# Layer 0's expert products in whole turns, and a staggered S5 loop, in a two-layer hybrid diffusion backbone

## The chip, the cores and the metric

The kernel runs on one core of one Trainium2 chip. The metric is the device time of one launch in microseconds, the median of three runs. TensorE multiplies, VectorE and ScalarE do most of the element-wise work, GpSimd does the rest of it and the indirect transfers, and SyncE issues nearly all loads. Each engine works through its own instructions strictly in the order in which they stand in the program; they wait for each other at semaphores.

## The reference

Two layers (DEPTH = 2), each a mixer followed by a mixture of experts, over 512 latent tokens and 256 context tokens of 1024 channels, all in float32. Layer 0 updates latents and context, layer 1 only the latents.

The mixer has four branches (attention, Mamba-2 SSD, S5, a gated short convolution) that are merged by sigmoid gates. The S5 branch has 24 groups of 16 inputs and 64 complex states, runs over the tokens in both directions, and is what the change touches:

```
ab_re, ab_im, bb_re, bb_im = s5_discretise(lam_re[d], lam_im[d], log_step[d], b_re, b_im)
h = complex_linear_scan(ab, s5_drive(u, bb))        # h[t] = ab*h[t-1] + bb@u[t], d = 1 on flipped tokens
y = Re(c @ (h_fwd + h_bwd)) + d_skip*u ;  y = gelu(y) ; y = y * sigmoid(y @ w_glu + b_glu)
```

The mixture is expert choice: each of 16 experts takes its best tokens, 64 of the latents and, in layer 0, 32 of the context.

```
aff = softmax(h @ w_router); gval, idx = top_k(aff.T, cap); xg = h[idx]
hid = silu(xg @ w_gate[e]) * (xg @ w_up[e]) ;  ye = (hid @ w_down[e]) * gval ;  out[idx] += ye
```

Each of the three weight matrices of an expert is 1024 x 1024, so 12 MiB are loaded for each expert and layer.

## The kernel before

**Experts.** `wtile()` loads half a matrix per tile `we`. There are two streams ("jobs"): latents (64 tokens, the 1024 output columns in 2 parts of 512) and, in layer 0, context (32 tokens, 4 parts of 256). The two tilings are "64-column" (2 parts at once beside each other in the array) and "32-column" (4 parts). `up()` (products on L1346) multiplies a stream by gate or up weights, 8 chunks of the inner dimension, k = 0 to 7. `hidden()` makes silu(g)*u on ScalarE and VectorE (L1357 to L1359), transposes it on TensorE (L1362) and copies it out of PSUM on ScalarE (hidT, L1364). `down()` multiplies by the down weights (L1376). Between them stand the gathers of the next tokens: `pick` (L1301) and the transposes of the gathered rows (L1332). In the code an expert (after expert 0) has gate for both streams, up for both streams, the hidden layers, then down for both.

PSUM has 8 banks, dealt among three groups by a triple: 'a', 'b', 'mm' (shown as psa, psb, psmm). `MIX = ((2, 3, 3), (3, 3, 2))` is that of the mixer of layers 0 and 1, `MOE` has the same numbers. In layer 0 an expert takes from group 'a' a bank for the latents' gate, one for both of the context's products, one for the latents' up, and one for the latents' down. `self.va(n, tag)` takes the next bank of a group, in turn; without a tag it is 'b' in S5.

**S5.** The loop `for g0 in range(0, 24, 4)` runs six times over four groups. In an iteration: the products Bx = B*powers (six GpSimd instructions, the helper's L995 to L1000) and Cx = C*powers (six on VectorE, the same lines; ScalarE negates one part, L1129); transposes of Bx (TensorE L1134, copied to Bt by ScalarE L1135); the short kernel matrix KK (TensorE L1143, sums L1147 to L1149 on ScalarE and VectorE), spread to T0 by DMA; the transposed inputs U (TensorE L1157, ScalarE L1158) and their copy in reversed order Ur (VectorE L1159, L1160); the driven inputs pv (TensorE L1165, L1166); the phase tables T (GpSimd, six instructions); H = T*pv (VectorE L1177 to L1182), the scan (VectorE L1185), S = the states turned back (VectorE L1192 to L1196); the readout y = T0*U + Cx*S (TensorE L1201, L1203), and its sum into u_tok (VectorE L1207). Every tile of the loop has one buffer, so the next iteration's T can be written only after the last L1193.

While S5 runs, TensorE also gets products of the input projections (L98 to L100, three for each product, in a split float32 form; fwL, L114 on VectorE, makes the low part of a weight) and of the modulation (L193 to L214). They fill TensorE between S5's own products.

**What sets the order.** The program is laid out when it is built. A scheduler goes through the instructions with a cost model of its own and appends to each engine's program the one that it holds ready first; the order in the code breaks ties. So the two streams of an expert, and the filling products of S5, stand in the order which that model finds, not in that of the code, unless a dependency is given by hand.

Of the kernel before, what the change touches and what calls it, by code (L numbers as in the profile page):

```python
# [9 lines left out]
F32 = mybir.dt.float32  # L10
# [45 lines left out]
MOE = ((2, 3, 3), (3, 3, 2))  # L56


class Kern:
# [942 lines left out]
    def s5(self):  # L1002
        nc, wp, par = self.nc, self.wp, self.par
# [113 lines left out]
        with self.pool("s5b") as bp:  # L1117
            W = lambda nm, *s: bp.tile([128, *s], F32, name=nm)
            for g0 in range(0, 24, 4):
                gg = slice(g0, g0 + 4)  # L1120

                Bx = [W(f"Bx{i}", 4, 8, 16) for i in range(2)]
                Cx = [W(f"Cx{i}", 4, 10, 16) for i in range(2)]
                z1, e1 = W("z1", 4, 10, 16), W("e1", 4, 8, 16)
                ap = lambda P, n, i: P[:, i, :, gg].rearrange("p s g -> p g s")[:, :, :, None].to_broadcast([128, 4, n, 16])
                av = lambda v, n: v[:, gg][:, :, None, :].to_broadcast([128, 4, n, 16])
                self.cmul(nc.gpsimd, Bx[0], Bx[1], ap(PB, 8, 0), ap(PB, 8, 1), av(bb[0], 8), av(bb[1], 8), e1)
                self.cmul(V, Cx[0], Cx[1], ap(PC, 10, 0), ap(PC, 10, 1), av(cc[:, 0], 10), av(cc[:, 1], 10), z1)
                nc.scalar.mul(Cx[1], Cx[1], -1.0)  # L1129
                Bt = [W(f"Bt{i}", 4, 128) for i in range(2)]  # L1130
                for i in range(2):
                    ps = self.va(512)
                    for q in range(4):
                        nc.tensor.transpose(ps[:, q * 128:(q + 1) * 128], Bx[i][:, q].rearrange("p s i -> p (s i)"), self.ident)  # L1134
                    nc.scalar.copy(Bt[i].rearrange("p a b -> p (a b)"), ps)  # L1135

                KK = bp.tile([16, 4, 15, 16], F32, name="KK")
                kf = [self.va(128).rearrange("p (d j) -> p d j", d=8) for _ in range(2)]
# [15 lines left out]
                U, Ur = W("U", 4, 96), W("Ur", 4, 96)  # L1154
                ps = self.va(384).rearrange("p (g b) -> p g b", g=4)
                for q in range(4):
                    nc.tensor.transpose(ps[:, q], u_tok[:, g0 + q].rearrange("p s i -> p (s i)"), self.ident[:96, :96])  # L1157
                nc.scalar.copy(U, ps)  # L1158
                V.tensor_copy(Ur[:, :, 0:32], U[:, :, 31::-1])  # L1159
                V.tensor_copy(Ur[:, :, 32:96], U[:, :, 95:31:-1])  # L1160
                pv = []
                for i in range(2):
                    p = self.va(384).rearrange("p (g b) -> p g b", g=4)
                    for q in range(4):
                        nc.tensor.matmul(p[0:64, q], Bt[i][:, q, 0:64], U[:, q], start=True, stop=True, skip_group_check=True)  # L1165
                        nc.tensor.matmul(p[64:128, q], Bt[i][:, q, 64:128], Ur[:, q], start=True, stop=True, skip_group_check=True)  # L1166
                    pv.append(p)

                T = [W(f"Tr{i}", 4, 6, 16) for i in range(2)]
                h4 = lambda i: hi[:, i, :, gg].rearrange("p a g -> p g a")[:, :, :, None].to_broadcast([128, 4, 6, 16])  # L1170
                l4 = lambda i: lo[:, i, 1:17, gg].rearrange("p a g -> p g a")[:, :, None, :].to_broadcast([128, 4, 6, 16])
                self.cmul(nc.gpsimd, T[0], T[1], h4(0), h4(1), l4(0), l4(1), e1[:, :, :6])
                T = [x.rearrange("p g a b -> p g (a b)") for x in T]

# [7 lines left out]
                V.tensor_sub(H[1], H[1], g2)  # L1182
# [468 lines left out]
```

## Time and profile before

| what | value |
|---|---|
| median of 3 runs | 3123.74 us (3120.9 to 3125.51) |
| profiled execution | 3125.83 us, of which the span of the trace 3124.1 us |
| TensorE (PE), VectorE (DVE), ScalarE, GpSimd busy | 2846.2, 1559.2, 783.8, 619.7 us (91, 50, 25, 20%) |
| granted TensorE clock, mean | 0.966 of full speed |
| bytes moved by DMA, mean rate | 659.79 MB, 211 GB/s |
| S5 loop of layer 0 and of layer 1 | 385 to 564.4 us, 2055 to 2241.8 us |
| experts of layer 0; experts 1 to 5; 6 to 15 | 1131.7 to 1733.4; 1172.3 to 1346.9; to 1733.4 us |
| experts of layer 1 | from about 2650 us to the end |

The stages follow each other in time: the projections, SSD and S5 of layer 0, attention, merge, experts, then the same for layer 1. The busy shares are averages over stages of different kinds. A row of windows has the stretch, its length, busy time and count of PE, PEld (weight loads, beside PE), DVE, ACT and POOL, the granted clock, the DMA share and GB/s. In a timeline the count of TensorE's float32 products is twice that of the program's instructions, as the trace has two records for each. What stands in brackets is the idle time ahead of an instruction and what ended it.

### The profile page before, as it was taken

The numbers are of one execution on the slowest core, as the hardware profiler recorded it, in microseconds if no ns is written. First come the engines' busy times: TensorE is split into PE (matmuls) and PEld (weight loads), VectorE is DVE, ScalarE is ACT, GpSimd is POOL, SyncE is SP. The second block draws the span as 40 slices with busy tenths as digits, with TensorE's granted clock in tenths as the row PEclk, the third lists the DMA queues.
The fourth block names the chain that finished last, engine by engine and source line by source line (L and its number), as shares of the span: only waits on it lengthen the run. The fifth ranks groups of instructions, "written<-read, shape, count | busy, mean of one in ns | idle before, by whom it ended". The sixth has DMA issues, their size and how long they took to land. (4 is left out here: it accounts for less than half of the span.)

```text
span 3124.1 us, 47057 instructions
## 1 busy us (share of the span) xinstructions
PE 2846.2 (91%) x18626; PEld 1826.3 (58%) x18626; DVE 1559.2 (50%) x3507; ACT 783.8 (25%) x1725; POOL 619.7 (20%) x765
## 2 busy tenths in 40 slices
PE   7999878999999979999999799977999896998887
PEld 4866756788888943433333376756687684332223
DVE  5477688555436552212111546798856565232223
ACT  4253222426522200000000332322436421000001
POOL 1022165120004121111110104065220031010001
PEclk9999999999999989999999899988999997999999
DMA  7324424311256479999996531432320486999998
GB/s 234 116 69 132 139 89 124 120 48 53 79 199 200 155 278 396 402 383 351 339 363 254 183 110 54 153 105 75 98 76 25 162 283 254 409 408 409 409 409 305
DMA packets 323039, 659.79 MB, mean 211 GB/s; under 512 B 22017, under 2 KB 191233, under 8 KB 322818
## 3 DMA queue, kind: packets, MB, share of 16 engines
q1 hardware_dynamic: 300688, 601.66, 53.6%
q10 hardware_dynamic: 15186, 32.93, 2.8%
q0 software_dynamic: 6944, 22.19, 2.3%
q8 instruction: 147, 2.41, 0.3%
q14 instruction: 74, 0.61, 0.1%
HBM read 602.85 MB, written 50.71 MB: 209 GB/s over the span
## 5 line engine op out<-in xcount | busy, mean ns | idle before, releaser
L1346 PE MATMUL psa<-we,X 128*64 128x512 f32 (+1 forms) x4096 | 605.1, 494 | 31.2 <-DMA we<-in_w_exp_gate_dram 15.8
L1346 PEld LDWEIGHTS psa<-we,X 128*64 128x64 f32 (+1 forms) x4096 | 193.7, 123 | 422.9 <-issue 318.7
L98 PE MATMUL psmm<-hH,fwH 128*128 128x512 f32 x984 | 374.1, 380 | 7.8 <-DVE xpad L636 3.6
L100 PE MATMUL psmm<-hH,fwL 128*128 128x512 f32 x984 | 368.3, 374 | 0.0
L99 PE MATMUL psmm<-hL,fwH 128*128 128x512 f32 x984 | 368.2, 374 | 0.0
L1376 PE MATMUL psa<-we,hidT 128*64 128x512 f32 x992 | 248.7, 609 | 21.3 <-ACT hidT L1364 14.9
L98 PEld LDWEIGHTS psmm<-hH,fwH 128*128 128x128 f32 x984 | 190.8, 194 | 51.4 <-issue 14.6
L1357 ACT ACTIVATE hid<-psa 128x512 f32<-128x512 f32 (+1 forms) x48 | 25.3, 526 | 779.1 <-PE psa L1346 739.3
L100 PEld LDWEIGHTS psmm<-hH,fwL 128*128 128x128 f32 x984 | 190.6, 194 | 30.7 <-issue 5.9
L99 PEld LDWEIGHTS psmm<-hL,fwH 128*128 128x128 f32 x984 | 191.1, 194 | 29.2 <-issue 6.1
L1381 DVE SCALAR_TENSOR_TENSOR y<-psa,ag,m 64x512 f32<-64x512 f32 x62 | 46.5, 750 | 274.0 <-PE psa L1376 273.4
L1376 PEld LDWEIGHTS psa<-we,hidT 128*64 128x64 f32 x992 | 67.8, 138 | 156.9 <-issue 112.5
L1359 DVE TENSOR_TENSOR hid<-hid,psa 128x512 f32<-128x512 f32 (+1 forms) x48 | 28.7, 597 | 252.1 <-PE psa L1346 251.8
L114 DVE TENSOR_TENSOR fwL<-fr,fwH 128x1024 fp32r<-128x1024 f32 (+1 forms) x100 | 117.1, 1172 | 73.4 <-ACT fwH L113 64.6
L471 POOL TENSOR_TENSOR merged<-merged,tgm 128x512 f32<-128x512 f32 (+1 forms) x48 | 62.8, 1326 | 424.0 <-DVE tgm L469 423.7
L1337 POOL TENSOR_TENSOR X<-X,modT 128x512 f32<-128x512 f32 x40 | 42.4, 1073 | 491.3 <-DVE X L1336 474.9
L1358 DVE SCALAR_TENSOR_TENSOR hid<-hid,psa 128x512 f32<-128x512 f32 (+1 forms) x48 | 28.7, 598 | 221.8 <-ACT hid L1357 221.8
L98 PE MATMUL psa<-cwH,hH 128*128 128x256 f32 (+1 forms) x432 | 122.1, 283 | 0.1
L113 ACT CAST fwH<-fr 128x1024 fp32r<-128x1024 f32 (+1 forms) x100 | 89.6, 897 | 128.2 <-DMA fr<-in_w_in_dram 62.1
L100 PE MATMUL psa<-cwH,hL 128*128 128x256 f32 (+1 forms) x432 | 121.6, 282 | 0.0
L99 PE MATMUL psa<-cwL,hH 128*128 128x256 f32 (+1 forms) x432 | 121.3, 281 | 0.0
L416 ACT ACTIVATE tg<-psmm 128x512 f32<-128x512 f32 x96 | 51.2, 533 | 160.4 <-PE psmm L100 152.8
(528 smaller groups left out, 5879.1 us busy)
## 6 DMA issues: line engine op xcount, KB each, us to landing
we<-in_w_exp_gate_dram SPq DMA_DIRECT2D x128, 1024.0 KB
we<-in_w_exp_up_dram SPq DMA_DIRECT2D x128, 1024.0 KB
we<-in_w_exp_down_dram SPq DMA_DIRECT2D x128, 1024.0 KB
fr<-in_w_mod_dram SPq DMA_DIRECT2D x96, 512.0 KB
fr<-in_w_in_dram SPq DMA_DIRECT2D x64, 512.0 KB
raw<-in_w_in_dram SPq DMA_DIRECT2D x36, 512.0 KB
gs<-tg ACTq DMA_DIRECT2D x32, 384.0 KB
tgm<-gs SPq DMA_DIRECT2D x32, 384.0 KB
```

The lines of the kernel that those rows point to most:

```text
L98: self.nc.tensor.matmul(ps, ah, bh, start=start and i == 0, stop=False)
L99: self.nc.tensor.matmul(ps, ah, bl, start=False, stop=False)
L100: self.nc.tensor.matmul(ps, al, bh, start=False, stop=stop and i == n - 1)
L113: self.nc.scalar.copy(h, x)
L114: self.nc.vector.tensor_sub(l, x, h.bitcast(F32))
L416: nc.scalar.activation(tg[:, o:o + n], self.cm(w, m, o, n), AF.Tanh, scale=0.5)
L471: (V if i == 3 else nc.gpsimd).tensor_add(dst, dst, t)
L1337: nc.gpsimd.tensor_add(X[:, hk], X[:, hk], Bm[:, 24 + h * 4:28 + h * 4, s:s + 1].to_broadcast([128, 4, 128]))
L1346: self.lastup = nc.tensor.matmul(ps[s][j * c:(j + 1) * c], X[s][:, k, r:r + c], w(k)[:, j * n:(j + 1) * n], start=k == 0, stop=k == 7, ski ...
L1358: V.scalar_tensor_tensor(hid, hid, 1.0, g, op0=OP.add, op1=OP.mult)
L1376: nc.tensor.matmul(ps[j * c:(j + 1) * c], lh, w(k)[:, j * n:(j + 1) * n], start=k == 0, stop=k == 7, skip_group_check=True)
L1381: V.scalar_tensor_tensor(Y[s][r, nn], ps[j * c:(j + 1) * c], got[s][1][r, e:e + 1], m5[s][r, nn], op0=OP.mult, op1=OP.mult)
```

## The change

Two parts, which share no instruction.

**Experts of layer 0.** `MOE[0]` becomes (4, 2, 2): four banks in group 'a', two in each of the others. Up now runs with the context ahead of the latents (`jobs[::-1]`), so that the 32-column products of gate and up follow each other. `behind()` adds a dependency that costs no semaphore (both instructions are TensorE's) and ties the first product of a turn behind the last product of the turn before, in gate, up and down.

**S5.** The iteration is split into `drive(g0)` (Bx, Bt, U, Ur, pv) and `matrices(g0)` (T, Cx, KK, T0). The drive of the next four groups is written right after H, ahead of the scan, and the next matrices right after the readout. U has two buffers. Ur is made by two ScalarE copies straight from PSUM, in reversed order, in place of VectorE's copies of U. The transposes of U and Bx, the products of KK and the readout take their banks from group 'a' (2 banks in layer 0, 3 in layer 1); pv stays in 'b'.

```diff
-MOE = ((2, 3, 3), (3, 3, 2))
+MOE = ((4, 2, 2), (3, 3, 2))
...
+            def drive(g0):
...
+                self.cmul(nc.gpsimd, Bx[0], Bx[1], ap(PB, 8, 0, gg), ap(PB, 8, 1, gg), av(bb[0], 8, gg), av(bb[1], 8, gg), e1)
+                U, Ur = bp.tile([128, 4, 96], F32, name="U", bufs=2), W("Ur", 4, 96)
+                ps = self.va(384, "a").rearrange("p (g b) -> p g b", g=4)
+                for q in range(4):
+                    nc.tensor.transpose(ps[:, q], u_tok[:, g0 + q].rearrange("p s i -> p (s i)"), self.ident[:96, :96])
+                nc.scalar.copy(U, ps)
+                nc.scalar.copy(Ur[:, :, 0:32], ps[:, :, 31::-1])
+                nc.scalar.copy(Ur[:, :, 32:96], ps[:, :, 95:31:-1])
...
-                    ps = self.va(512)
+                    ps = self.va(512, "a")
...
+            def matrices(g0):
...
+                self.cmul(nc.gpsimd, T[0], T[1], h4(0), h4(1), l4(0), l4(1), e1[:, :, :6])
+                self.cmul(V, Cx[0], Cx[1], ap(PC, 10, 0, gg), ap(PC, 10, 1, gg), av(cc[:, 0], 10, gg), av(cc[:, 1], 10, gg), z1)
...
-                kf = [self.va(128).rearrange("p (d j) -> p d j", d=8) for _ in range(2)]
+                kf = [self.va(128, "a").rearrange("p (d j) -> p d j", d=8) for _ in range(2)]
...
-                V.tensor_copy(Ur[:, :, 0:32], U[:, :, 31::-1])
-                V.tensor_copy(Ur[:, :, 32:96], U[:, :, 95:31:-1])
...
+            nxt, mats = drive(0), matrices(0)
+            for g0 in range(0, 24, 4):
+                gg = slice(g0, g0 + 4)
+                (U, pv), (Cx, T0, T) = nxt, mats
...
                 V.tensor_sub(H[1], H[1], g2)
+                if g0 < 20:
+                    nxt = drive(g0 + 4)
...
+                if g0 < 20:
+                    mats = matrices(g0 + 4)
...
+            def behind(ins, first):
+
+                tc.add_manual_dep(ins.ins, first.ins.name, mybir.DependencyInfo(mybir.DependencyClass.NoSync, mybir.DependencyReason.DATA))
...
+                            if s and k + j == 0:
+                                behind(ins, last_)
...
-                    for job in jobs:
-                        up(wg, X, pg, job, e, side)
+
+                    turns = [(wg, pg, job) for job in jobs]
                     wu = wtile()
-                    for job in jobs:
-                        up(wu, X, pu, job, e, side)
+                    turns += [(wu, pu, job) for job in jobs[::-1]]
+                    for i, (w, p, job) in enumerate(turns):
+                        up(w, X, p, job, e, side, self.lastup if i and both else None)
```

**Where instructions move.** The first place is TensorE in an expert of layer 0, before, in the experts from 6 on: the end of the gate and up products, and down. X_14760 are the latents' rows (64x512 products), X_14340 the context's (32x256); hid and hidT are the hidden layers and their transposes.

```order
L1346 MATMUL psa<-we,X_14760 64x512 x4
L1346 MATMUL psa<-we,X_14340 32x256 x8
L1362 MATMUL psb<-cst,hid_14960 128x128 x4
L1376 MATMUL psa<-we,hidT_14969 64x512
L1362 MATMUL psb<-cst,hid_14971 128x128 x2
L1376 MATMUL psa<-we,hidT_14969 64x512 x3
L1376 MATMUL psb<-we,hidT_14978 32x256
L1376 MATMUL psa<-we,hidT_14969 64x512 x4
L1376 MATMUL psb<-we,hidT_14978 32x256 x12
L1376 MATMUL psa<-we,hidT_14969 64x512 x4
L1376 MATMUL psb<-we,hidT_14978 32x256 x11
```

The eight pairs of 4 and 8 ahead of these rows look like the first two of them: the streams alternate after each half of a weight tile, in down too. The same engine after the change, one expert of the same stretch (xg are gathered rows; L1363, L1381, L1395 and L1345 answer to L1346, L1362, L1376 and L1332):

```order
L1363 MATMUL psa<-we,X_13411 64x512 x16
L1363 MATMUL psa<-we,X_13445 32x256 x56
L1345 MATMUL psmm<-cst,xg_13437 128x128 x8
L1363 MATMUL psa<-we,X_13445 32x256 x8
L1363 MATMUL psa<-we,X_13411 64x512 x16
L1381 MATMUL psb<-cst,hid_13643 128x128 x4
L1381 MATMUL psb<-cst,hid_13654 128x128 x2
L1395 MATMUL psa<-we,hidT_13652 64x512 x16
L1395 MATMUL psb<-we,hidT_13661 32x256 x32
```

Each stream's products now stand in one piece, the context's for gate and up in a single one, and both transposes of the hidden layers stand together ahead of down; in the experts 1 to 5 the order before had whole turns as well, with the context's up products last.

The second place is VectorE in S5 of layer 0, before, from the sum into u_tok of one iteration to H of the next.

```order
L1207 TENSOR_TENSOR u_tok<-u_tok,psb 96x512
L997 TENSOR_TENSOR Cx_2907<-Cx_2907,z_2909 128x640
L998 TENSOR_TENSOR Cx_2908<-PC,cc 128x640
L999 TENSOR_TENSOR z_2909<-PC,cc 128x640
L1000 TENSOR_TENSOR Cx_2908<-Cx_2908,z_2909 128x640
L1159 COPY Ur<-U 128x4x32
L1160 COPY Ur<-U 128x4x64
L114 TENSOR_TENSOR fwL<-fr,fwH 128x1024
L1177 TENSOR_TENSOR Vr_3014<-Tr_3006,psb 128x384
L1148 TENSOR_TENSOR KK<-KK,psb 16x16
L1181 TENSOR_TENSOR g_3017<-Tr_3007,psb 128x384
```

After, at the same place, from the last S of one iteration on (L1186 and L1190 are H, L1220 would be the sum into u_tok):

```order
L1207 TENSOR_TENSOR S_3086<-g_3018,g_3019 64x4x64
L1186 TENSOR_TENSOR Vr_3175<-Tr_3118,psb 128x384
L996 TENSOR_TENSOR z_3116<-PC,cc 128x640
L114 TENSOR_TENSOR fwL<-fr,fwH 128x1024
L1190 TENSOR_TENSOR g_3178<-Tr_3119,psb 128x384
L203 TENSOR_REDUCE modT_165<-psmm 128x4
L204 TENSOR_TENSOR modT_165<-modT_165,bmT 128x4
L211 TENSOR_TENSOR br<-br,psmm 2x256
L214 TENSOR_SCALAR br<-br 2x256
L995 TENSOR_TENSOR Cx_3114<-PC,cc 128x640
L998 TENSOR_TENSOR Cx_3115<-PC,cc 128x640
L997 TENSOR_TENSOR Cx_3114<-Cx_3114,z_3116 128x640
```

The copies Ur are gone from this engine; two of H's products stand ahead of Cx and of the sum into u_tok, so they wait for GpSimd's T and no longer for what TensorE does in that iteration. The third place is TensorE in the same loop, before, where U's transposes and the first products pv stand.

```order
L1143 MATMUL psb<-Cx_2907,bbr 32x128 x2
L1157 MATMUL psb<-cst,u_tok 128x96 x4
L99 MATMUL psmm<-hL,fwH 128x256
L100 MATMUL psmm<-hH,fwL 128x256
L98 MATMUL psmm<-hH,fwH 128x256
L99 MATMUL psmm<-hL,fwH 128x256
L100 MATMUL psmm<-hH,fwL 128x256
L1165 MATMUL psb<-U,Bt_2924 64x96
L98 MATMUL psmm<-hH,fwH 128x256
```

And after, where the transposes of Bx and the first products pv stand, an iteration ahead of their use:

```order
L100 MATMUL psmm<-hH,fwL 128x256
L98 MATMUL psmm<-hH,fwH 128x256
L99 MATMUL psmm<-hL,fwH 128x256
L1139 MATMUL psa<-cst,Bx_3026 128x128 x4
L1139 MATMUL psa<-cst,Bx_3027 128x128 x4
L100 MATMUL psmm<-hH,fwL 128x256
L98 MATMUL psmm<-hH,fwH 128x256
L1145 MATMUL psb<-U,Bt_3045 64x96
L1146 MATMUL psb<-Ur,Bt_3045 64x96
```

The products pv were split by filling products, with those that take U and those that take Ur apart; now they stand together behind the transposes. Counted over the whole program, the filling products L98 to L100 that stand ahead of the last readout become 1091 where they were 1068 in layer 0, and 799 where they were 748 in layer 1.

## Rows read from the trace of the kernel before

**Rows 1.** Windows: span, busy PE PEld DVE ACT POOL, PEclk, DMA share, GB/s

```profile
385.00:564.40 179.40, 150.96 (x1199) 114.35 (x1199) 152.15 (x252) 46.43 (x108) 103.23 (x96) 0.92 0.35 106
...
2055.00:2241.80 186.80, 150.70 (x988) 112.98 (x987) 160.89 (x245) 53.17 (x107) 108.44 (x97) 0.89 0.28 83
...
2650.00:3124.00 474.00, 405.92 (x1876) 143.42 (x1872) 128.58 (x233) 40.34 (x88) 34.97 (x41) 0.98 0.99 392
```

**Rows 2.** Windows of layer 0's experts 1 to 5, then 6 to 15

```profile
1172.30:1346.90 174.60, 173.79 (x1504) 69.83 (x1500) 38.26 (x83) 9.71 (x20) 30.48 (x28) 1.00 1.03 398
1346.90:1733.40 386.50, 380.02 (x2996) 126.52 (x2993) 70.07 (x132) 20.02 (x41) 46.61 (x47) 1.00 0.88 327
```

**Rows 3.** TensorE timeline, expert 2: start, time, instructions, [idle before, releaser]

```profile
1206.92 21.29 PE L1346 MATMUL psa<-we,X 128*64 128x512 f32 x192
...
1230.95 7.08 PE L1376 MATMUL psa<-we,hidT 128*64 128x512 f32 x30
...
1241.56 0.65 PE L1346 MATMUL psa<-we,X 128*64 128x512 f32 x2
```

**Rows 4.** TensorE timeline of expert 9, same columns

```profile
1464.04 23.50 PE L1346 MATMUL psa<-we,X 128*64 128x512 f32 x192
```

**Rows 5.** TensorE timeline of layer 1, first expert, one stream

```profile
2815.77 0.66 PE L1362 MATMUL psb<-cst,hid 128*128 128x128 f32 x4 [0.79 <-DVE hid L1359]
2817.11 7.09 PE L1376 MATMUL psa<-we,hidT 128*64 128x512 f32 x32 [0.68 <-ACT hidT L1364]
```

**Rows 6.** S5's first five iterations and the last, layer 0, then 1

```profile
385.00:540.90 155.90, 127.82 (x1001) 95.98 (x1000) 134.54 (x210) 38.76 (x91) 101.49 (x95) 0.91 0.32 98
540.90:564.40 23.50, 23.14 (x204) 18.37 (x199) 17.61 (x44) 7.67 (x19) 1.73 (x1) 1.00 0.52 157
...
2055.00:2219.60 164.60, 128.94 (x833) 96.42 (x831) 142.36 (x207) 42.80 (x88) 107.10 (x96) 0.88 0.27 79
2219.60:2241.80 22.20, 21.76 (x158) 16.55 (x157) 18.53 (x40) 10.38 (x20) 1.34 (x1) 1.00 0.39 113
```

**Rows 7.** TensorE's waits in S5 (total, times, longest), both layers

```profile
PE psb L1166 <- DVE Ur L1160: 14.2, 6, 4.5
...
PE psb L1166 <- DVE Ur L1160: 13.4, 6, 4.5
PE psb L1203 <- DVE S L1196: 12.7, 5, 4.0
```

**Rows 8.** VectorE's groups (busy, mean ns, idle before), S5, both layers

```profile
L1159 DVE COPY Ur<-U 128x128 f32<-128x128 f32 x6 | 5.9, 987 | 2.4 <-ACT U L1158 2.4
...
L1160 DVE COPY Ur<-U 128x256 f32<-128x256 f32 x6 | 3.4, 574 | 0.0
...
L1159 DVE COPY Ur<-U 128x128 f32<-128x128 f32 x6 | 5.8, 961 | 1.2 <-ACT U L1158 1.2
L1160 DVE COPY Ur<-U 128x256 f32<-128x256 f32 x6 | 4.9, 821 | 0.0
```

**Rows 9.** ScalarE's groups in S5 of layer 0

```profile
L1158 ACT COPY U<-psb 128x384 f32<-128x384 f32 x6 | 2.9, 480 | 8.8 <-PE psb L1157 8.7
```

**Rows 10.** VectorE timeline without GpSimd at work, then beside it

```profile
542.19 0.81 DVE L998 TENSOR_TENSOR Cx<-PC,cc 128x640 f32<-128x640 f32 x1
...
451.07 1.73 DVE L998 TENSOR_TENSOR Cx<-PC,cc 128x640 f32<-128x640 f32 x1
```

**Rows 11.** TensorE timeline in S5: filling products, then a wait

```profile
454.19 0.39 PE L98 MATMUL psmm<-hH,fwH 128*128 128x512 f32 x1
454.42 0.40 PE L99 MATMUL psmm<-hL,fwH 128*128 128x512 f32 x1
...
459.82 0.30 PE L1166 MATMUL psb<-Ur,Bt 128*64 128x96 f32 x1 [4.54 <-DVE Ur L1160]
```

**Rows 12.** GpSimd timeline in S5 of layer 0

```profile
473.54 1.39 POOL L995 TENSOR_TENSOR Tr<-hi,lo 128x384 f32<-128x384 f32 x1 [12.65 <-DVE g L1192]
...
478.72 1.46 POOL L1000 TENSOR_TENSOR Tr<-Tr,e 128x384 f32<-128x384 f32 x1
```

More of the change, by code (lines that the diff above doesn't have):

```diff
@@ L1118, in s5 @@
             W = lambda nm, *s: bp.tile([128, *s], F32, name=nm)
-            for g0 in range(0, 24, 4):
+            av = lambda v, n, gg: v[:, gg][:, :, None, :].to_broadcast([128, 4, n, 16])
+            ap = lambda P, n, i, gg: P[:, i, :, gg].rearrange("p s g -> p g s")[:, :, :, None].to_broadcast([128, 4, n, 16])
+            def drive(g0):
                 gg = slice(g0, g0 + 4)
                 Bx = [W(f"Bx{i}", 4, 8, 16) for i in range(2)]
[L1123 to L1129, printed above, removed]
+                e1 = W("e1", 4, 8, 16)
+                self.cmul(nc.gpsimd, Bx[0], Bx[1], ap(PB, 8, 0, gg), ap(PB, 8, 1, gg), av(bb[0], 8, gg), av(bb[1], 8, gg), e1)
[6 more added lines that the diff above has]
+                nc.scalar.copy(Ur[:, :, 32:96], ps[:, :, 95:31:-1])
                 Bt = [W(f"Bt{i}", 4, 128) for i in range(2)]
                 for i in range(2):
-                    ps = self.va(512)
+                    ps = self.va(512, "a")
                     for q in range(4):
@@ L1135, in s5 @@
                     nc.scalar.copy(Bt[i].rearrange("p a b -> p (a b)"), ps)
+                pv = []
+                for i in range(2):
+                    p = self.va(384).rearrange("p (g b) -> p g b", g=4)
+                    for q in range(4):
+                        nc.tensor.matmul(p[0:64, q], Bt[i][:, q, 0:64], U[:, q], start=True, stop=True, skip_group_check=True)
+                        nc.tensor.matmul(p[64:128, q], Bt[i][:, q, 64:128], Ur[:, q], start=True, stop=True, skip_group_check=True)
+                    pv.append(p)
+                return U, pv
+            def matrices(g0):
+                gg = slice(g0, g0 + 4)
+                Cx = [W(f"Cx{i}", 4, 10, 16) for i in range(2)]
+                z1, e1 = W("z1", 4, 10, 16), W("e1", 4, 8, 16)
+                T = [W(f"Tr{i}", 4, 6, 16) for i in range(2)]
+                h4 = lambda i: hi[:, i, :, gg].rearrange("p a g -> p g a")[:, :, :, None].to_broadcast([128, 4, 6, 16])
+                l4 = lambda i: lo[:, i, 1:17, gg].rearrange("p a g -> p g a")[:, :, None, :].to_broadcast([128, 4, 6, 16])
+                self.cmul(nc.gpsimd, T[0], T[1], h4(0), h4(1), l4(0), l4(1), e1[:, :, :6])
+                self.cmul(V, Cx[0], Cx[1], ap(PC, 10, 0, gg), ap(PC, 10, 1, gg), av(cc[:, 0], 10, gg), av(cc[:, 1], 10, gg), z1)
+                nc.scalar.mul(Cx[1], Cx[1], -1.0)
                 KK = bp.tile([16, 4, 15, 16], F32, name="KK")
-                kf = [self.va(128).rearrange("p (d j) -> p d j", d=8) for _ in range(2)]
+                kf = [self.va(128, "a").rearrange("p (d j) -> p d j", d=8) for _ in range(2)]
                 for d in range(2):
@@ L1152, in s5 @@
                     nc.sync.dma_start(T0[s * 16:(s + 1) * 16], KK[:, :, 7 - s:15 - s].rearrange("p g d j -> p g (d j)"))
[L1154 to L1158, printed above, removed]
-                V.tensor_copy(Ur[:, :, 0:32], U[:, :, 31::-1])
-                V.tensor_copy(Ur[:, :, 32:96], U[:, :, 95:31:-1])
[L1161 to L1173, printed above, removed]
+                return Cx, T0, [x.rearrange("p g a b -> p g (a b)") for x in T]
+            nxt, mats = drive(0), matrices(0)
+            for g0 in range(0, 24, 4):
+                gg = slice(g0, g0 + 4)
+                (U, pv), (Cx, T0, T) = nxt, mats
                 H = [W(f"Vr{i}", 4, 96) for i in range(2)]
@@ L1196, in s5 @@
                     V.tensor_tensor(S[i][64:128, :, 95:31:-1], g1[64:128, :, 31:95], g2[64:128, :, 31:95], op=op)
-                ps = self.va(512)[:96]
+                ps = self.va(512, "a")[:96]
                 for q in range(4):
@@ L1338, in rows, with up @@
                 return X
-            def up(w, X, ps, job, e, side):
+            def behind(ins, first):
+                tc.add_manual_dep(ins.ins, first.ins.name, mybir.DependencyInfo(mybir.DependencyClass.NoSync, mybir.DependencyReason.DATA))
+            def up(w, X, ps, job, e, side, first=None):
                 s, c, parts, o = job
@@ L1347, in up @@
                                          skip_group_check=True)
+                        if first is not None and k + j == 0:
+                            behind(self.lastup, first)
                     if k % 4 == 3:
```

5 lines of the change are left out of this document (3 added, 2 removed).

## The prediction

> **What bounds the kernel now.** I read the windows by stage first. Three stretches matter. The S5 loops take 179.4 and 186.8 us; in each neither TensorE nor VectorE is busy all the time (151 and 152 us in layer 0, 151 and 161 in layer 1), so the loop is bound by the two waiting for each other. Layer 1's experts run at a DMA share of 0.99: they are bound by their weights and begin earlier or later, but don't get shorter [rows 1]. Layer 0's experts are TensorE's: from expert 1 on it is busy 173.8 of 174.6 us and 380.0 of 386.5 [rows 2]. Those two rows also show what the first part of the change is about: experts 1 to 5 take 174.6 / 5 = 34.92 us each, experts 6 to 15 take 386.5 / 10 = 38.65, though they do the same work.
>
> Next the timelines of TensorE. The 192 records of gate and up take 21.29 us in expert 2 [rows 3] and 23.50 in expert 9 [rows 4], with no idle time inside either. The order shown above has the reason: in expert 9 the 64- and the 32-column products alternate after each half of a weight tile, 15 changes of tiling against 3, so (23.50 - 21.29) / 12 = 0.18 us for a change. Down alternates as well, which with its waits is the rest of the 3.7 us.
>
> Then the waits inside S5. TensorE's largest is for the reversed inputs Ur: 14.2 and 13.4 us, up to 4.5 at a time; in layer 1 also 12.7 us for S [rows 7]. I split each loop at the sum into u_tok: five iterations with GpSimd at work take 155.9 and 164.6 us, VectorE busy 134.5 and 142.4 in them; the last, with nothing to prepare, takes 23.5 and 22.2 [rows 6].
>
> **The experts of layer 0.** The order after has whole turns in experts 1 to 15. I price an expert from one that has them already, 34.92 us, and correct for what else moves.
> - The 32-column turns of gate and up join: one change less, -0.18 (by the price above).
> - The latents' up is now last, so their product with silu, their transposes and the copy hidT are no longer covered by the context's up. The row with nothing to cover them is layer 1's first expert: 0.79 us idle ahead of the transposes, and from these to the first product of down 2817.11 - 2815.77 = 1.34 [rows 5], together 2.13. Before, the stretch from the last up product to the main run of down was, in expert 2, 1230.95 - (1206.92 + 21.29) = 2.74 us, in which two products of down (2 x 7.08 / 30 = 0.47) were already done, so 2.27, gathered rows' transposes and a pick among it [rows 3]. After, gathered rows and picks stand at those same gaps in most experts and can lie in the idle 0.79 and 0.68. If all of them are covered the stretch is 2.27 - 2.13 = 0.14 shorter. If none is, it is longer by at most what of the 2.27 is not transposes of the hidden layers (0.66 for one set [rows 5]): 1.6.
>
> So an expert takes between 34.92 - 0.18 - 0.14 = 34.6 and 34.6 + 1.6 = 36.2. I take 34.7, since most are covered. Experts 6 to 15 give 10 x (38.65 - 34.7) = 39.5, experts 1 to 5 give 5 x 0.22 = 1.1, expert 0 nothing: **-40 us**, bounds -18 (10 x 2.45 - 5 x 1.28) and -42 (10 x 4.05 + 5 x 0.32). The bank (4, 2, 2) allows this order and costs nothing by itself: down's and the context's banks no longer wait for VectorE to empty the gate's.
>
> What is late next there is the weights. They come at 398 GB/s where TensorE takes an expert in 34.9 us, without a wait, and at 327 where it takes 38.7 [rows 2]; 12 MiB in 34.7 us is 363 GB/s. I take the lower rate as less demand, as TensorE's wait list of that stretch names no transfer of weights.
>
> **S5.** VectorE loses the copies Ur: 5.9 + 3.4 = 9.3 us in layer 0, 5.8 + 4.9 = 10.7 in layer 1 [rows 8]. ScalarE gets two copies out of PSUM instead. No row has a reversed read by ScalarE; the nearest is its copy of the same 128x384, 0.48 us [rows 9], and from the other side VectorE's reversed copies, 0.57 to 0.99 each [rows 8]. Six times 0.5 to 2 us on an engine busy 46 of 179 us, an iteration ahead of its use, costs nothing.
>
> The waits are the larger part. TensorE's for Ur go, as pv is made a whole iteration early. In their place come three: TensorE for Cx, with KK ahead of the next drive; U's and Bx's transposes for one of two 'a' banks, which are free when VectorE has added KK; and VectorE's second product of H for T, which GpSimd starts when S has read the old one and ends 478.72 + 1.46 - 473.54 = 6.64 us later [rows 12], with the last writes of S, one product of H, one of Cx and often an fwL of VectorE's between, by the order above. VectorE is idle 155.9 - 134.5 = 21.4 and 164.6 - 142.4 = 22.2 us in the five iterations [rows 6]. I let a third of it go: 155.9 - 9.3 - 7.1 = 139.5 and 164.6 - 10.7 - 7.4 = 146.5, that is -16.4 and -18.1. The last iterations stay.
>
> The loops also take more filling products, 23 and 51. One costs 454.42 - 454.19 = 0.23 us of TensorE [rows 11]: 5.3 and 11.7 us, which make TensorE's part of the five iterations at most 127.8 + 5.3 = 133 and 128.9 + 11.7 = 141, still under 139.5 and 146.5. They are taken out of later stretches in which TensorE is nearly always busy: -16 (I count 5.3 + 11.7, less a tenth). S5 together: -16.4 - 18.1 - 16 = **-50 us**. Bounds: if all idle time stays, -9.3 - 10.7 - 16 = -36; if TensorE's own work is all that is left, (155.9 - 133) + (164.6 - 141) + 16 = -62.
>
> One thing speaks against even that. The same VectorE product, 128x640 with two inputs in SBUF, takes 0.81 us with GpSimd silent and 1.73 beside it [rows 10], and an iteration without GpSimd has 17.6 us of VectorE against 134.5 / 5 = 26.9 [rows 6]. So time in which VectorE now stands idle is time in which GpSimd runs freely; when the gaps close, the two meet more often, and what VectorE gains in waits it may lose in longer instructions. That is the end at -36, which I keep as a case of its own.
> The Trainium skill (SBUF — State Buffer, "Who interferes with whom") says so outright: an instruction of VectorE with two inputs in SBUF and one of GpSimd that reads SBUF hold the shared port in turn, each for its whole length. The trace agrees in the 0.81 and 1.73 us above; by that rule alone S5 would bring 36 us and not 50.
>
> **Sum.** The profiled execution took 3125.8 us, 1.7 more than its span and 2.1 more than the median of the runs. 3125.8 - 40 - 50 = 3035.8, and with the median's 2.1 less, **3034 us**. All of it comes ahead of layer 1's experts, whose transfers start when the stage before gives up its space, so none is lost there.
>
> **Rivals.**
> - GpSimd eats the waits (above): -40 - 36, 3048 us. For it: VectorE's durations beside GpSimd. Against: ScalarE's and TensorE's part of the waits is not VectorE's at all. Chance 0.20.
> - Only the experts pay. The S5 loops are bound by a ring through Cx, KK's banks and T that is as long as the old one; -40, 3084 us. For it: each wait removed has one in its place. Against: pv and Bx are a full iteration early. Chance 0.11.
> - Only S5 pays. The 327 GB/s of experts 6 to 15 is what the loads manage there, so whole turns wait for weights; -50, 3074 us. For it: that row alone. Against: 398 in the same stage, no DMA among the waits for weights. Chance 0.07.
> - Slower. In S5, T's 6.6 us, a wait of TensorE for banks as long as the longest one seen (4.5) and the old idle time (4.4) all lie end to end with VectorE's (134.5 + 142.4 - 20) / 10 = 25.7: 41.2 us an iteration against 32.05, ten times +9.2 = +92. With the experts' -40 and the products' -16 this gives 3160 us. It decides from 5.6 us an iteration on. For it: two banks for six uses an iteration. Against: 25.7 us of VectorE in which TensorE can catch up. Chance 0.07.
> - The gains and that loss cancel, about 5 us an iteration: no change. Chance 0.05.
>
> **Numbers.** My forecast has 0.50, between 3010 and 3045. Faster holds it and the first three rivals: 0.88; 0.2% (6 us, about what a measurement of this kernel can tell) either side of none 0.05; slower 0.07. The range reaches below to S5 at its bound with the experts' (3125.8 - 2.1 - 42 - 62 = 3020) and, as those bounds come from one execution's means, 20 us more, 3000, and above past the case in which only the experts pay, 3090.
>
> **What would show it.** Right: experts 6 to 15 at 34.6 to 35 us each, each stream's products in one piece; no wait for Ur; VectorE about 9 us less busy in each S5 loop, which end after some 163 and 169 us. Wrong: waits of layer 0's TensorE for weights; VectorE's H waiting for T by microseconds; L995 to L1000 longer on VectorE than before; TensorE standing at the transposes of U or Bx behind KK.

## The result and the profile after

The changed kernel takes 3076.78 us (median, 3075.18 to 3079.53) against 3124.62 (3120.9 to 3127.23): a ratio of 0.9849, interval 0.9832 to 0.9866, or 48 us less. 3034 was forecast, 90 less; the way and the range hold, the size is about half, and the time lies outside 3010 to 3045, which I held likeliest. The first part brought its 40 us almost to the microsecond, the second brought 5 to 8 in place of 50.

First the windows of the experts of layer 0 after, experts 1 to 5 and 6 to 15; they answer to [rows 2].

```profile
1172.70:1344.80 172.10, 168.49 (x1506) 69.76 (x1502) 42.32 (x84) 9.21 (x20) 30.78 (x29) 1.00 1.03 400
1344.80:1693.70 348.90, 336.82 (x2996) 138.05 (x2992) 72.75 (x134) 19.66 (x42) 45.06 (x46) 1.00 0.95 364
```

172.1 / 5 = 34.4 us and 348.9 / 10 = 34.9 us an expert, where it was 34.92 and 38.65. All fifteen take 521.0 us in place of 561.1. The loads followed: 364 GB/s in the second row, which was 327. Next TensorE's timeline of expert 9, which answers to [rows 4, 5].

```profile
1451.54 21.15 PE L1363 MATMUL psa<-we,X 128*64 128x512 f32 x192
1473.48 0.87 PE L1381 MATMUL psb<-cst,hid 128*128 128x128 f32 x6 [0.79 <-DVE hid L1378]
1474.29 0.39 PE L1314 MATMUL psmm<-slotT,pick 16*128 16x512 bf16 x1
1474.87 7.09 PE L1395 MATMUL psa<-we,hidT 128*64 128x512 f32 x32 [0.19 <-ACT hidT L1383]
...
1485.48 0.65 PE L1363 MATMUL psa<-we,X 128*64 128x512 f32 x2
```

The same 192 records take 21.15 us in place of 23.50, with 2 changes of tiling where there were 15: (23.50 - 21.15) / 13 = 0.18 us each, the price that I had from the kernel before. Counted over all experts of layer 0 in the traces, gate, up and down together change between the two tilings 267 times before and 63 times after: 204 changes at 0.18 us are 37 of the 40 us. (The Trainium skill, TensorEngine Tiling (Array Packing), "Key Properties", has the rule that a change of tiling mode drains TensorE; it gives no figure. That a change costs time is what the trace shows with these 0.18 us; a drain as such is not seen in it.) Behind them stand the two waits that the new order lays open: 0.79 us for the product of the hidden layer, exactly as in layer 1's row, and 0.19 for its copy, as a pick (L1314) fills part of the time between.

Now S5, the loops of both layers and then layer 1's experts, at the places that answer to [rows 1] (the second is moved by as much as the experts ahead of it got shorter).

```profile
385.00:564.60 179.60, 148.71 (x1176) 112.07 (x1176) 147.64 (x242) 49.43 (x117) 101.11 (x94) 0.90 0.35 107
2015.30:2196.80 181.50, 151.36 (x1020) 116.61 (x1013) 160.61 (x260) 55.03 (x119) 107.80 (x97) 0.90 0.32 95
2593.20:3077.80 484.60, 414.88 (x1906) 146.00 (x1906) 130.53 (x237) 40.42 (x88) 37.97 (x45) 0.98 0.99 390
```

Layer 0's loop takes 179.6 us, as before. Layer 1's takes 181.5 where it took 186.8. VectorE is indeed 4.5 us less busy in layer 0, but not in layer 1 (160.6 against 160.9). Layer 1's experts, which before begin at 2640.9 us, have their old length but for 1.4 us, bound by DMA at 0.99:

```profile
2640.90:3124.10 483.20, 415.00 (x1906) 146.27 (x1906) 130.45 (x237) 40.34 (x88) 38.11 (x45) 0.98 0.99 391
```

VectorE lost copies of 9.3 and 10.7 us [rows 8], but only 4.5 and 0.3 us of busy time. A good part of what is missing went into its scan of the states, whose 48 instructions take 5 to 6 us longer in each layer's loop; here are those of layer 0 before, then after.

```profile
L1185 DVE TENSOR_TENSOR_SCAN Vr<-rho,Vr 128x96 f32<-128x96 f32 x48 | 15.8, 391 | 0.0
```

```profile
L1196 DVE TENSOR_TENSOR_SCAN Vr<-rho,Vr 128x96 f32<-128x96 f32 x48 | 21.5, 497 | 0.0
```

Of the 96 scans of both layers 4 overlap an instruction of GpSimd before and 29 after. Without one beside it a scan takes 0.33 us in both traces; beside one it takes 0.81 on average after. The reversed copies cost ScalarE little, in the groups of layer 0's loop after (they answer to [rows 9]):

```profile
L1134 ACT COPY Ur<-psa 128x256 f32<-128x256 f32 x5 | 1.9, 378 | 0.1
L1133 ACT COPY Ur<-psa 128x128 f32<-128x128 f32 x5 | 1.4, 271 | 0.0
```

The largest waits of TensorE in the two loops after, layer 0 and then layer 1 (total, times, longest); they answer to [rows 7].

```profile
PE psa L1167 <- DVE Cx L997: 7.4, 3, 3.2
PE psa L1139 <- ACT KK L1173: 6.6, 3, 5.1
PE psmm L208 <- DVE modT L203: 5.7, 2, 5.1
PE psa L1139 <- POOL Bx L997: 4.2, 1, 4.2
```

```profile
PE psa L1167 <- DVE Cx L997: 16.4, 6, 6.2
PE psmm L208 <- DVE modT L203: 3.5, 2, 3.2
PE psa L1139 <- POOL Bx L1000: 2.7, 1, 2.7
```

The waits for Ur (14.2 and 13.4 us) are gone, and that for S in layer 1 fell from 12.7 to 2.5. In their place TensorE waits longer for Cx ahead of KK, and in layer 0 for KK's bank ahead of Bx's transposes; it waits for Bx itself as well. The wait for the sums modT of the modulation is not new. The same two waits before, layer 0 and then layer 1:

```profile
PE psmm L208 <- DVE modT L203: 8.3, 2, 5.0
PE psb L1143 <- DVE Cx L997: 2.4, 1, 2.4
```

```profile
PE psb L1143 <- DVE Cx L997: 2.5, 3, 2.0
PE psmm L208 <- DVE modT L203: 2.0, 1, 2.0
```

In all TensorE stands idle 30.9 us in layer 0's loop, where it was 28.4, and 30.1 in layer 1's, where it was 36.1 (length less busy time, in the windows above and [rows 1]). So what S5's part gains lies in layer 1. From layer 0's last down product to layer 1's first expert product the traces have 899.4 us after and 898.8 in s5_only (below), against 903.6 to 910.3 in the four kernels that have S5 as before. Up to layer 0's first expert product those four take 1128.0 to 1131.8 us, and the two with the new S5 1132.9 and 1127.6, with TensorE's order the same in both: no difference that these traces could tell.

### The profile page after: what moved, and what is told of

Its sections match the earlier page's. It is cut to its first block, busy times and chain, and to the rows that moved or that the text cites. A ratio compares the mean times of both kernels' runs of the same rounds, so it can differ in the third digit from the quotient of the medians.

```text
span 3077.8 us, 47019 instructions
## 1 busy us (share of the span) xinstructions
PE 2786.8 (91%) x18626; PEld 1830.8 (59%) x18626; DVE 1552.3 (50%) x3483; ACT 787.2 (26%) x1749; POOL 615.4 (20%) x765
## 5 line engine op out<-in xcount | busy, mean ns | idle before, releaser
L1363 PE MATMUL psa<-we,X 128*64 128x512 f32 (+1 forms) x4096 | 582.1, 491 | 34.1 <-DMA we<-in_w_exp_gate_dram 17.3
L1363 PEld LDWEIGHTS psa<-we,X 128*64 128x64 f32 (+1 forms) x4096 | 204.1, 124 | 388.3 <-issue 274.6
L98 PE MATMUL psmm<-hH,fwH 128*128 128x512 f32 x984 | 374.9, 381 | 8.4 <-DVE xpad L636 3.6
L100 PE MATMUL psmm<-hH,fwL 128*128 128x512 f32 x984 | 370.2, 376 | 2.2 <-DVE fwL L114 2.2
L1395 PE MATMUL psa<-we,hidT 128*64 128x512 f32 x992 | 229.9, 603 | 19.3 <-ACT hidT L1383 14.2
L98 PEld LDWEIGHTS psmm<-hH,fwH 128*128 128x128 f32 x984 | 191.6, 195 | 51.2 <-issue 12.3
L100 PEld LDWEIGHTS psmm<-hH,fwL 128*128 128x128 f32 x984 | 192.0, 195 | 34.2 <-issue 7.1
L1376 ACT ACTIVATE hid<-psa 128x512 f32<-128x512 f32 (+1 forms) x48 | 25.3, 526 | 654.4 <-PE psa L1363 615.5
L1377 DVE SCALAR_TENSOR_TENSOR hid<-hid,psa 128x512 f32<-128x512 f32 (+1 forms) x48 | 28.7, 599 | 271.0 <-ACT hid L1376 271.0
L1395 PEld LDWEIGHTS psa<-we,hidT 128*64 128x64 f32 x992 | 68.1, 138 | 157.8 <-issue 112.9
L1378 DVE TENSOR_TENSOR hid<-hid,psa 128x512 f32<-128x512 f32 (+1 forms) x48 | 28.7, 599 | 195.6 <-PE psa L1363 195.0
L98 PE MATMUL psa<-cwH,hH 128*128 128x256 f32 (+1 forms) x432 | 122.8, 284 | 1.1 <-DVE R L905 0.9
L100 PE MATMUL psa<-cwH,hL 128*128 128x256 f32 (+1 forms) x432 | 122.0, 282 | 0.0
```

The costliest lines, as they stand in the source:

```text
L98: self.nc.tensor.matmul(ps, ah, bh, start=start and i == 0, stop=False)
L100: self.nc.tensor.matmul(ps, al, bh, start=False, stop=stop and i == n - 1)
L1363: self.lastup = nc.tensor.matmul(ps[s][j * c:(j + 1) * c], X[s][:, k, r:r + c], w(k)[:, j * n:(j + 1) * n], start=k == 0, stop=k == 7, ski ...
L1377: V.scalar_tensor_tensor(hid, hid, 1.0, g, op0=OP.add, op1=OP.mult)
L1395: ins = nc.tensor.matmul(ps[j * c:(j + 1) * c], lh, w(k)[:, j * n:(j + 1) * n], start=k == 0, stop=k == 7, skip_group_check=True)
```

## The experiments

All are timed against the kernel before on the same chip, in three groups on three chips; where two experiments are compared, it is by their ratios to it. The first two part the change.

**moe_only**: the changed kernel with S5 as before.

```diff
-            nxt, mats = drive(0), matrices(0)
             for g0 in range(0, 24, 4):
...
+                V.tensor_copy(Ur[:, :, 0:32], U[:, :, 31::-1])
```

> Only the experts' part of the change; S5 as before. If the experts pay by themselves (theory A: 40 us from experts 1 to 15, at 34.73 us each as in the changed kernel's trace) the time is 3124.6 - 40 = 3085 us, and S5's part is worth the rest, some 7 us. If the experts' gain in the changed kernel leans on S5's part (theory B, by what stands in TensorE's queue when they begin) it is under 30 us, above 3094.

3083.61 us, ratio 0.9874 (0.9857 to 0.9892): 39 us less than before. Theory A holds.

**s5_only**: the kernel before with S5's part.

```diff
+            nxt, mats = drive(0), matrices(0)
             for g0 in range(0, 24, 4):
...
-                V.tensor_copy(Ur[:, :, 0:32], U[:, :, 31::-1])
```

> Only S5's part of the change; the experts as before. By theory A (S5's staggered loop gives back what it takes) 3117 us, 5 to 9 under before, layer 0's loop within 3 us of before and layer 1's 5 us shorter. By the prediction's sum S5 is worth 50 us: 3075.

3116.77 us, ratio 0.9984 (0.9975 to 0.9993): about 5 us less. The two parts add up to the whole within the intervals (0.0126 + 0.0016 against 0.0151), so neither hides the other.

**moe_tied_oldbanks** and **moe_untied** part the experts' change: the first has the ties and the reversed up, but the banks of before, the second the new banks and the reversed up, but no ties. The edits are shown against moe_only.

```diff
 moe_tied_oldbanks:
-MOE = ((4, 2, 2), (3, 3, 2))
+MOE = ((2, 3, 3), (3, 3, 2))
 moe_untied:
-                        up(w, X, p, job, e, side, self.lastup if i and both else None)
+                        up(w, X, p, job, e, side)
-                                behind(ins, last_)
+                                pass
```

> As moe_only (the experts' part alone), but with the old banks (2, 3, 3). If the fixed order is what pays (theory A), the banks are worth nothing, as each bank has been read during the turn ahead of its next use: 3080 to 3087, with 34.7 us an expert. If the four banks are needed for the order, the latents' up waits for the gate's bank: 1 us or more an expert, over 3098.

3077.93 us, ratio 0.9861 (0.9841 to 0.988): all of the gain without the banks.

> As moe_only, with the new banks and the context ahead of the latents in up, but without the ties between the turns. The streams then alternate again in the order from the experts on that alternated before (theory A: 12 changes of tiling more in gate and up, some 10 in down, 0.18 us each, about 4 us an expert): 3112 to 3124. If the banks or the reversed jobs were what pays: 3080 to 3095.

3113.48 us, ratio 0.9973 (0.9962 to 0.9984): 8 of the 39 us stay (6 by the medians). TensorE's timeline of this kernel, around one expert:

```profile
1410.29 1.94 PE L1382 MATMUL psa<-we,hidT 128*64 128x512 f32 x8
1412.16 1.49 PE L1382 MATMUL psb<-we,hidT 128*32 128x256 f32 x20
1413.58 1.94 PE L1382 MATMUL psa<-we,hidT 128*64 128x512 f32 x8
1415.44 2.78 PE L1382 MATMUL psb<-we,hidT 128*32 128x256 f32 x42
```

The down products alternate, 8 records of 64 columns and 20 to 42 of 32, as they did before, and gate and up alternate again as well. Counted as above, this kernel changes the tiling 213 times in layer 0's experts, 54 fewer than before, and 54 x 0.18 = 9.7 us is about what these experts gain in its trace (590.6 us from the first product to the last, against 601.2). So the time goes with the number of changes: what pays is the order of the turns, and the ties hold it. The banks are worth nothing that these runs could tell. A kernel with the ties but without the reversed up was not run; by the price above its one change more an expert would cost 15 x 0.18 = 2.7 us, an estimate.

**ur_dve**: the reversed inputs back on VectorE.

```diff
-                nc.scalar.copy(Ur[:, :, 0:32], ps[:, :, 31::-1])
-                nc.scalar.copy(Ur[:, :, 32:96], ps[:, :, 95:31:-1])
+                V.tensor_copy(Ur[:, :, 0:32], U[:, :, 31::-1])
+                V.tensor_copy(Ur[:, :, 32:96], U[:, :, 95:31:-1])
```

> The changed kernel, but the reversed inputs Ur are copied by VectorE from U again, not by ScalarE from PSUM. If VectorE's instructions set the loops' pace, this costs the 9 to 11 us a loop that the copies take: 3077 + 20 = 3097. If the ring over Cx and the readout sets it and VectorE has idle time in it, it costs under 8: up to 3085.

3075.95 us, ratio 0.9851 (0.9836 to 0.9866), the same as the change. That the copies, 9 to 11 us a loop, are off VectorE, a term of my sum, is worth nothing that these runs could tell.

**readout_t0**: the readout reads T0 where it read Cx, so that Cx of the next groups need not wait for it.

```diff
-  nc.tensor.matmul(o, S[i][:, q], Cx[i][:, q, 1:9].rearrange("p s j -> p (s j)"), start=False, stop=i == 1)
+  nc.tensor.matmul(o, S[i][:, q], T0[:, q], start=False, stop=i == 1)
```

> The changed kernel, but the readout multiplies the states by T0 in place of Cx (same sizes and count), so that the next group's Cx need not wait until the readout has read the old one; this leaves out the readout's true weights. Theory R: the loop is a ring readout, Cx, KK, H, scan, S, readout on one buffer of Cx; then VectorE's wait at its first Cx product for the readout (10.1 and 4.1 us, and 6.2 and 1.7 at the sum into u_tok) and TensorE's wait for Cx ahead of KK (7.4 and 16.4 us) shrink by half or more and the time falls by 15 to 30 us, to 3047 to 3062. Rival G: VectorE's longer instructions beside GpSimd set the pace; then the waits move elsewhere and the time is within 6 us of 3077.

3085.65 us, ratio 0.9883 (0.9868 to 0.9898): slower than the change by 0.0034, some 10 us, although VectorE no longer waits for the readout ahead of Cx (10.1 us in layer 0's loop in the change, none here). TensorE's waits ahead of KK (L1167), which theory R wanted halved, grew in layer 0's loop from 8.2 us (7.4 above, and 0.8 for ScalarE's part of Cx) to 23.6. This miss is the key to the case. The windows below are, for each kernel, layer 0's S5 loop and everything from the start to the first expert; before first.

```profile
380.00:565.10 185.10, 156.66 (x1213) 118.71 (x1213) 157.57 (x263) 46.43 (x108) 107.99 (x98) 0.91 0.35 107
0.00:1131.70 1131.70, 1039.25 (x7063) 847.90 (x7063) 700.39 (x1658) 400.12 (x920) 265.20 (x351) 0.97 0.40 128
```

The changed kernel:

```profile
380.00:565.30 185.30, 154.41 (x1227) 116.95 (x1216) 153.21 (x250) 51.79 (x124) 105.81 (x97) 0.91 0.36 111
0.00:1132.90 1132.90, 1035.86 (x7063) 845.13 (x7063) 697.56 (x1646) 402.78 (x932) 262.80 (x351) 0.97 0.40 128
```

readout_t0:

```profile
380.00:548.50 168.50, 126.84 (x1054) 98.12 (x1047) 145.82 (x239) 46.44 (x114) 108.64 (x97) 0.86 0.29 89
0.00:1139.80 1139.80, 1035.88 (x7061) 847.67 (x7061) 695.08 (x1646) 403.88 (x932) 268.94 (x351) 0.96 0.40 127
```

In readout_t0 the loop is 185.3 - 168.5 = 16.8 us shorter than in the change, and yet the experts begin 6.9 us later. TensorE did 126.8 us of work in the loop where it did 154.4; the filling products that found no room there were done afterwards. Up to the first expert TensorE has the same work in all three (7061 to 7063 records), so what counts is when it has done it, and that is its busy time plus its idle time up to that point. Idle it is 1131.7 - 1039.3 = 92.4 us before, 97.0 after, 103.9 in readout_t0. The first two can't be told apart: over the traces of the kernels with the old S5 this idle time is 88.6 to 93.8 us, and s5_only, with the new one, has 91.6. That of readout_t0 lies above all of them, and the 16.8 us by which its loop is shorter gained nothing.

**no_cx**: Cx made for the first four groups only.

```diff
+                if g0 == 0:
+                    self.cmul(V, Cx[0], Cx[1], ap(PC, 10, 0, gg), ap(PC, 10, 1, gg), av(cc[:, 0], 10, gg), av(cc[:, 1], 10, gg), z1)
+                    nc.scalar.mul(Cx[1], Cx[1], -1.0)
+                    keep.extend(Cx)
+                Cx = keep
```

> The changed kernel, but the products Cx are made once, for the first four groups, and used for all (this leaves out the true weights of the other groups). It takes 30 us a loop off VectorE and the waits of TensorE for Cx (8 us in layer 0, 19 in layer 1). Theory I: the time falls by about these waits, 20 to 30 us, to 3047 to 3057, although VectorE loses 60 us of work and the loops get far shorter. By the prediction's way of counting (the loop's length is what is gained) it would fall by 50 or more, under 3027.

3053.74 us, ratio 0.9792 (0.9776 to 0.9809). The same two windows:

```profile
380.00:531.80 151.80, 122.40 (x1058) 95.69 (x1058) 124.47 (x217) 41.56 (x107) 94.77 (x97) 0.90 0.33 99
0.00:1119.70 1119.70, 1027.33 (x7063) 843.86 (x7063) 672.58 (x1616) 401.23 (x927) 251.21 (x351) 0.97 0.40 129
```

The loop is 33.5 us shorter than in the change and the experts begin 13.2 us earlier. TensorE's idle time up to there is 92.4, 4.6 us less than after; the other 8.5 us are the same records in less busy time (1027.3 against 1035.9), for which the rows show no cause: the granted clock is 0.97 in both. Over all traces the busy time of these records is 1027 to 1041 us, so it moves by as much as the idle time does. Theory I holds roughly for the size (18 us by the ratios, 23 by the medians), but idle time is only part of how it came; the prediction's way of counting, by the loop's length, is out.

**sel_first**: the row product of the modulation ahead of its transposes, so that it shares no wait with VectorE's sum.

```diff
+            part, jj = divmod(j, 4)
+            if part in (2, 5):
+                pr = pb[:32, 256:]
+                nc.tensor.matmul(pr, self.cst["sel"], row, start=True, stop=True, skip_group_check=True)
             for b in range(2):
                 nc.tensor.transpose(pt[:, b].rearrange("p q c -> p (q c)"), row[:, b * 128:(b + 1) * 128], self.ident)
...
-            part, jj = divmod(j, 4)
             if part in (2, 5):
-                pr = pb[:32, 256:]
-                nc.tensor.matmul(pr, self.cst["sel"], row, start=True, stop=True, skip_group_check=True)
```

> The changed kernel with one other thing: in the modulation the product for the row form (the old L208) stands ahead of the two transposes whose sums VectorE takes, so TensorE no longer waits there until VectorE has read the bank (5.7 us in layer 0's S5, 7.4 in layer 1's). Theory I: all that S5 can give is TensorE's idle time, since its filling products are done sooner or later anyway; then this gives 7 to 13 us, 3064 to 3070. Rival: the loop is a ring of waits in which another takes the place of the one removed: 3074 to 3080.

3066.18 us, ratio 0.983 (0.9814 to 0.9847): some 6 us better than the change by the ratios, whose intervals overlap a little, 10.6 by the medians. What it mends can be seen in the change's own trace, and stood in the kernel before too (8.3 us in layer 0, above). VectorE and then TensorE in the second iteration of layer 0:

```profile
444.50 1.18 DVE L996 TENSOR_TENSOR z<-PC,cc 128x640 f32<-128x640 f32 x1
445.61 2.01 DVE L114 TENSOR_TENSOR fwL<-fr,fwH 128x1024 fp32r<-128x1024 f32 x1
447.55 0.54 DVE L1190 TENSOR_TENSOR g<-Tr,psb 128x384 f32<-128x384 f32 x1
448.01 0.16 DVE L203 TENSOR_REDUCE modT<-psmm 128x4 f32<-128x16 f32 x1
...
456.80 0.82 DVE L995 TENSOR_TENSOR Cx<-PC,cc 128x640 f32<-128x640 f32 x1 [6.72 <-PE psa L1214]
```

```profile
440.16 0.38 PE L201 MATMUL psmm<-cst,row 128*128 128x128 f32 x2
...
448.23 1.06 PE L208 MATMUL psmm<-row,cst 128*32 128x256 f32 x2 [5.11 <-DVE modT L203]
...
454.08 0.50 PE L1212 MATMUL psa<-T,U 128*96 128x128 f32 x2
```

TensorE has transposed at 440.16, goes on with filling products, and then stands 5.11 us for VectorE's sum L203. That stands behind a product of Cx, an fwL of 2.01 us and H's product L1190, which the change put there ahead of the rest of Cx. So the readout comes at 454.08, and VectorE, which needs it read before it may overwrite Cx, stands idle 6.72 us. One wait made another.

**no_t**: T made for the first four groups only; **sel_t_dve**: sel_first with T made by VectorE.

```diff
 no_t:
+                if g0 == 0:
+                    self.cmul(nc.gpsimd, T[0], T[1], h4(0), h4(1), l4(0), l4(1), e1[:, :, :6])
+                    keep.extend(T)
+                T = keep
 sel_t_dve:
-                self.cmul(nc.gpsimd, T[0], T[1], h4(0), h4(1), l4(0), l4(1), e1[:, :, :6])
+                self.cmul(V, T[0], T[1], h4(0), h4(1), l4(0), l4(1), z1[:, :, :6])
```

> The changed kernel, but GpSimd makes the phase tables T once, for the first four groups (this leaves out the true tables of the others): 40 us less of GpSimd in a loop. If VectorE's longer instructions beside GpSimd are what keeps TensorE waiting for Cx (theory G), VectorE's Cx products come near 0.8 us each, TensorE's waits fall by 10 us or more in the two loops, and the time to 3055 to 3067. If not, it stays within 6 us of 3077.

3045.47 us, ratio 0.9761 (0.9744 to 0.9777), 27 us less than the change by the ratios and more than I expected.

> The changed kernel with the modulation's row product ahead and the phase tables T made by VectorE, no longer by GpSimd. Leaving T out gave 27 us less, though VectorE's gain was only some 13 us a loop. By theory G (GpSimd's work beside VectorE is what holds TensorE up) T costs VectorE 6 x 0.55 = 3.3 us an iteration and saves it as much or more in the Cx products: 3045 to 3062. If VectorE's work sets the pace, the 20 us a loop cost more than GpSimd's absence gives: 3066 to 3085.

3088.63 us, ratio 0.99 (0.9884 to 0.9916): theory G's forecast for this kernel fails. VectorE's product L998 of Cx in layer 0's loop, in the change, then in no_t (the same line), and TensorE's longest kind of wait in sel_t_dve:

```profile
L998 DVE TENSOR_TENSOR Cx<-PC,cc 128x640 f32<-128x640 f32 x6 | 8.9, 1489 | 0.0
```

```profile
L998 DVE TENSOR_TENSOR Cx<-PC,cc 128x640 f32<-128x640 f32 x6 | 5.9, 976 | 0.0
```

```profile
PE psa L1168 <- DVE Cx L998: 26.0, 5, 13.6
```

Without T on GpSimd the product takes 0.98 us where it took 1.49, so it does slow VectorE, as the prediction's case had it. But T on VectorE stands in the way of Cx, and TensorE waits 26.0 us for that. GpSimd's T costs less than the place it takes on VectorE. That does not refute theory G itself: in no_t TensorE's wait for VectorE's Cx ahead of KK, 7.4 and 16.4 us in the change, is gone in layer 0 and 2.7 us in layer 1. That fits the theory, though no_t also spares VectorE most of its waits for T. The rows agree with the Trainium skill's rule on the port that VectorE and GpSimd share (SBUF — State Buffer, "Who interferes with whom"), but the time that the prediction put on it did not come, neither S5's 36 us nor anything from moving T. In the traces no_t gains 16.6 us up to layer 0's first expert product and 9.1 between layer 0's last and layer 1's first; 8.0 and 8.5 of that are TensorE's idle time. The rest is less busy time for the same records, with the granted clock at 0.976 against 0.969 up to the first expert, and what brings it is not settled by these runs.

**kk_late** and **kk_sel**: KK and T0 behind the next drive in the code, alone and with sel_first's edit; `kernels()` is the part of `matrices()` that makes them.

```diff
                 if g0 < 20:
                     nxt = drive(g0 + 4)
+                T0 = kernels(g0, Cx)
```

> The changed kernel with KK moved behind the next drive in the code, so that TensorE has transposes and pv to do before it needs the new Cx. TensorE's wait at Bx's transposes for KK's bank (6.6 us in layer 0) should go. Theory I: the time changes by as much as TensorE's idle time in the two loops, whatever the loops' length; I expect 3 to 10 us less. Rival: with the filling products now all behind KK, TensorE waits longer for Cx, and the time is 3077 to 3090.

> A version meant to beat both: the changed kernel with the modulation's row product ahead of its transposes and KK behind the next drive. The two alone gave 3066.2 and 3069.9 (ratios to before 0.983 and 0.984 against the change's 0.985). If they take away different idle time of TensorE: 3055 to 3064. If it is the same: 3064 to 3070.

3069.92 us, ratio 0.9839 (0.9822 to 0.9855), and 3065.08 us, ratio 0.9824 (0.9808 to 0.984). The first can't be told from the change, the second is sel_first's time, as expected if the two take the same idle time. sel_first and kk_sel lie under the change by the median and the ratio, with intervals that overlap its own a little, and are the best complete versions that these runs point to. The rest of S5's waits (in sel_first for Cx above all) stays. A second buffer for Cx, which would be the direct test, wasn't tried.

## Why the prediction was half right

- **The experts**: right in mechanism and size. -40 forecast, 561.1 - 521.0 = 40.1 in the trace, 39 in moe_only. An expert was put at 34.7 us and takes 34.9 and 34.4. The mechanism, the changes of tiling, is borne out by their count in three kernels. That the banks allow the order was wrong: moe_tied_oldbanks has it without them. That loads would follow was right.
- **S5's waits**, forecast at -34 with the copies: this is the step that failed. I took idle time from VectorE (21.4 and 22.2 us), let a third go, and counted the loop's length as the gain. A shorter loop is no gain by itself, as readout_t0 shows, and TensorE, which the next stage waits for, stands idle as long as before in layer 0 (28.4 us, then 30.9; 28.7 in s5_only) and 6 us less in layer 1. There the whole gain of S5's part lies, 5 to 8 us, as far as these traces can tell. The waits for Ur turned into longer ones for Cx and into those for KK's bank and Bx. I had named Cx, KK's bank and T; I missed that Cx has to wait for the readout, and I passed over the wait for modT, which was layer 0's second largest before and stayed.
- **The copies Ur**, 9 to 11 us a loop: nothing (ur_dve). VectorE got 4.5 and 0.3 us less busy, where I gave about 9 as a sign.
- **The filling products**, -16: a wrong count. The 1091 and 799 that I gave count only those in group mm. Products of the same lines in group 'a' went the other way (48 and 72 fewer ahead of the last readout), so that in all 25 and 21 fewer stand there. TensorE's busy time in the loops is 148.7 us where it was 151.0, and 151.4 where it was 150.7: they hide no more of its work than before.
- **GpSimd as a rival**: its reason holds. VectorE's instructions meet GpSimd's more often (29 scans where it was 4) and give back part of what the copies freed; L995 to L1000 on VectorE, my sign for it, got shorter all the same (1.40, then 1.18 us on average in layer 0's loop). But S5 stayed far under its -36.
- **The rival that came**: only the experts pay, 3084 us, to which I gave 0.11. Its reason, a ring as long as the old one, fits the waits above, with one more link than I had, the readout; but breaking that link in readout_t0 did not shorten the time, so the ring is not shown to be what bounds S5.
- **The range** holds by its width: it was drawn past that rival. That is no merit of S5's sum; 3034 itself is 43 us off.

## What to carry to other kernels

A loop beside which an in-order TensorE works off filling products is not worth its length: look when the engine has done the same work, at the next stage that needs it, and price a change by the idle time that it takes from the engine up to there. Two traces of the same order differ too, here by 5 us up to layer 0's experts (after and s5_only), so a smaller difference between two traces settles nothing. A wait removed inside such a loop has to be followed to the next one in the same program order, and each product that the change puts earlier on an engine has to be asked what stands behind it. Where two tilings alternate, ties between whole turns give the time of the changes back.

## What the runs showed of the hardware that I had not expected

ScalarE reads PSUM in reversed order at no visible cost: 0.38 us for 128x256 and 0.27 for 128x128, beside 0.48 for the straight 128x384 [rows 9]. VectorE's scan of 128x96, 0.33 us by itself, takes 0.81 on average when an instruction of GpSimd overlaps it.
